# Values ahead of queries and keys in a retention mixer, two of their blocks as one double block with four sevens

## The chip, the core and the metric

The kernel runs on one core of a Trainium2 chip. TensorE (PE) multiplies matrices into PSUM; VectorE (DVE) and ScalarE (ACT) do elementwise work; GpSimd (POOL) takes a small part; SyncE (SP) issues most DMAs from HBM into SBUF. The metric is the device time in microseconds of one execution, the median of the runs.

## The reference

A decoder layer on 256 tokens of 2048 features, in float32: a half SwiGLU FFN, two token mixers side by side (retention over 8 heads, attention over a window of 128), a second half FFN, and a gated embedding, each followed by a layer norm. The change is in the retention mixer:

```
rq, rk, rv, rg, aq, ak, av, gate_r, gate_a = jnp.split(h @ w_in[i], SPLIT_POINTS, axis=-1)
rq = rotary(rq ...); rk = rotary(rk ...) * RET_DK ** -0.5
ro = head_group_norm(retention_chunkwise(rq, rk, rv), ret_gn_g[i])
ret_branch = (jax.nn.silu(rg) * ro) @ w_ret_out[i]
```

`rq` and `rk` have 1024 features each, the values `rv` 2048 (8 heads of 256). All of them are products of the same 256 x 2048 activations with columns of `w_in`. Queries, keys and values don't depend on each other; retention needs all three.

## The kernel before, in words

**A product.** Every float32 operand is split into a high part (rounded to the format that TensorE takes, `fp32r`, by an ACT cast, L98) and a low part (the rest, by a DVE subtraction, L99). A product is three matmuls: high by low, high by high, low by high (`Sum.add`, L393 to L395). Weights come in *chunks* of 128 x 1024 numbers, 512 KB; for values a chunk is two slices of 128 rows by 512 columns. A chunk against the two halves of the tokens is 12 matmuls of 512 columns.

**Pairs and sevens.** A *pair* is two slices of rows against two blocks of 512 columns and two halves of tokens, thus a 2 x 2 by 2 x 2 product of tiles. Plain ("P") it takes two chunks and 24 matmuls. A *seven* ("S", class `Seven`, L167) uses seven products in place of eight, 21 matmuls. It needs four sums of weight tiles (DVE, L189 to L192), the splits of both (class `Seven.make`), and on the left side four sums of activation tiles, the *forms* (`forms_of`, `whole` L478, `seven_forms` L466 to L469, and their split); one set of forms serves two sevens. After the last seven of a block, `seven_common` folds the shared products (ACT L500, DVE L501 to L504), and a last sum adds the plain part (L1438). `units_of("PPSSPSSP", (0, 1, 2, 3))` gives the order of units in a block and which row pairs are sevens. `mixer_block` runs such a double block; before, it serves the attention gates (`ga0`, `ga1`) and the retention output.

**The planner.** All weight units stand in one list, `plan`, in the order of their use (`plan_mixers` for this stage). `fill` moves them along: it issues loads (SyncE) while the queue of units, in units of time, is below `far`, and prepares them (ACT and DVE) while the prepared queue is below `ahead`, and only while slots are left: there are 46 slots of SBUF, and `slots_for_weights(n, ahead=45, far=90)` says how many the weights may hold. A single chunk counts 12, a seven 21. `done` frees a unit's slots and calls `fill`; so the instructions of preparing are written to DVE and ACT, which work in order, at that place of the program. During a layer norm `quiet` stops preparing; when the norm's last event "go" comes, the next `fill` prepares as much as the queue allows: 88 units after the first FFN (`last_ahead` 136, less 12 for each of 4 held chunks, in `held_out`).

**Lazy jobs.** Each unit used calls `run_side`, which also advances the first generator in `lazy` by a step. In this stage these are `sums_ahead` (sums and splits for sevens of the second FFN, L257 to L269, written away to HBM) and `rotary_table("a")`.

**The stage, before.** `mixers` takes block 0 of the values (`rv0`) inside the norm (`norm.first`, six chunks, then two more), splits the result into high and low slots (`values`, which the retention products read), and starts the lazy jobs. Then come eight groups of queries and keys (`rqk`, four chunks each, L344 and L352), each rotated on DVE (L1088 to L1098) into four slots `rq` and `rk`, the DMAs of the decay table (L1179), then values blocks 1, 2 and 3 one by one with `tokens_out`, each split from PSUM by `values`. Retention scores (L1193) begin one chunk into the next stage, `rg`.

Of the kernel before, what the change touches and what calls it, by code (L numbers as in the profile page):

```python
# [15 lines left out]
P = 128  # L16
# [39 lines left out]
def layer(ctx: ExitStack, tc: tile.TileContext, io):  # L56
# [13 lines left out]
    def banks(name):  # L70
        return [bank(name + str(j)) for j in range(2)]

    def slot(shape, dt, name):
        return slots.tile(shape, dt, tag="slot", name=name)
# [22 lines left out]
    def split(dst_hi, dst_lo, src, lo_engine=None):  # L97
        act.copy(dst_hi, src)  # L98
        (lo_engine or dve).tensor_tensor(dst_lo, src, dst_hi, ALU.subtract)  # L99
# [138 lines left out]
    def sums_ahead(items, wait, every):  # L238


        def pause():
            for _ in range(every):
                yield

        pairs = [[Chunk(k) for k in items[0]]]
        for _ in range(wait):
            yield
        for j, (key, _) in enumerate(items):
            a, b = pairs.pop()
            b11, b21, b12, b22 = a.of(a.raw, 0), a.of(a.raw, 1), b.of(b.raw, 0), b.of(b.raw, 1)  # L250
            u, v = (slot([P, 2, 512], F32, w + a.name) for w in "uv")
            t1, t3, t2, t4 = (x.rearrange("p (g n) -> p g n", g=2) for x in (u[:, 0], u[:, 1], v[:, 0], v[:, 1]))
            parts = [slot([P, 2, 512], F32R, w + a.name) for w in ("hu", "lu", "hv", "lv")]
            uh, ul, vh, vl = parts
            away = [dram.tile([P, 2, 512], F32, name=f"{w}{a.name}") for w in ("hud", "lud", "hvd", "lvd")]
            put_by_sums[key] = away
            dve.tensor_tensor(t1, b11, b12, ALU.add)  # L257
            dve.tensor_tensor(t3, b12, b22, ALU.add)
            yield from pause()
            act.copy(uh, u)  # L260
            dve.tensor_tensor(t2, b11, t3, ALU.add)
            dve.tensor_tensor(t4, t2, b21, ALU.add)
            yield from pause()
            act.copy(vh, v)
            if j + 1 < len(items):
                pairs.append([Chunk(k) for k in items[j + 1]])
            dve.tensor_tensor(ul, u, uh, ALU.subtract)
            yield from pause()
            dve.tensor_tensor(vl, v, vh, ALU.subtract)  # L269
            for e in range(2):  # L270
                sync.dma_start(away[e], parts[e].bitcast(F32))
            yield from pause()
            for e in range(2, 4):
                sync.dma_start(away[e], parts[e].bitcast(F32))
# [44 lines left out]
    def slots_for_weights(n, ahead=45, far=90):  # L319
        room.update(slots=n, ahead=ahead, far=far)  # L320
# [84 lines left out]
    def tokens_out(key, n_k, lhs, ps, n=512, before=None):  # L405

        nk = 1024 // n
        sums = [Sum(ps[t][:, :n], n_k) for t in range(2)]
        for c in range(n_k // nk):
            u = take(key + (c,))  # L410
            tokens_chunk(u.chunk, c * nk, lhs, sums, (0, 1), range(nk))
            done(u)
            run_side()
# [11 lines left out]
    def block(name, units, keys, lhs, forms, sums, fold, before=None):  # L425


        sevens = [p for kind, p in units if kind in "SD"]
        if sevens:
            p1, p6, p7, q5 = (Sum(bank(f"{name}s{j}"), len(sevens)) for j in range(4))  # L430
        for j, (kind, p) in enumerate(units):
            if before is not None:
                before(j)
            if kind in "PF":
                for n in range(2):
                    u = take(keys(n, p))
                    tokens_chunk(u.chunk, 2 * p, lhs, [sums[t][n] for t in range(2)], (0, 1))
                    done(u)
                    run_side()
                continue  # L440
            u = take(keys(0, p))
            a11, a12 = (half_of(lhs(2 * p + e), 0) for e in range(2))
            a22 = half_of(lhs(2 * p + 1), 1)
            f5, f6, f7, f3 = forms(p)
            q2, q3, q4 = sums[0][0], sums[0][1], sums[1][0]
            steps = [
                (p1, a11, u.b11), (q2, a12, u.b21), (q3, f3, u.b22), (q5, f5, u.t1),
                (p7, f7, u.t3), (p6, f6, u.t2), (q4, a22, u.t4),
            ]
            if p == sevens[-1]:  # L450
                steps = [steps[j] for j in (0, 3, 5, 4, 1, 2, 6)]
            for to, left, right in steps:
                to.add(left, right)
            done(u)
            run_side()
            if p == sevens[-1]:
                fold(p1.ap, p6.ap, p7.ap, q5.ap)
# [27 lines left out]
    def units_of(order, sevens, ahead=()):  # L485

        sevens, ahead = list(sevens), list(ahead)
        plain = [p for p in range(KD // 2) if p not in sevens + ahead]
        of = {"S": sevens, "D": ahead, "P": plain, "F": plain}
        return [(kind, of[kind].pop(0)) for kind in order]  # L490

    def block_sums(ps, units, n_k):

        s = sum(kind == "S" for kind, p in units)
        return [[Sum(ps[t][n], n_k - (2 * s if t and n else s)) for n in range(2)] for t in range(2)]
# [16 lines left out]
    def plan_tokens(key, n_k, nk=2):  # L512
        for c in range(n_k // nk):
            plan.append(Single(key + (c,)))
# [587 lines left out]

    GATE_UNITS = units_of("PPSSPSSP", (0, 1, 2, 3))
    RET_UNITS = units_of("PPPSPSPP", (0, 1))
    gate_keys = lambda b: lambda n, p: ("w_in_f2", 29 + 4 * b + 2 * n, p)
    ret_keys = lambda b: lambda n, p: ("w_ret2", 4 * b + 2 * n, p)

    def plan_mixers():
        plan_tokens(("w_rv", 0), KD)
        for grp in range(8):  # L1110
            plan_features([("w_in_f", grp)], KD)
        for blk in range(1, 4):
            plan_tokens(("w_rv", blk), KD)
        for grp in range(8, 16, 2):
            plan_tokens(("w_in_f2", grp), KD)
        plan_tokens(("w_av",), KD, nk=4)
        for grp in (20, 16, 17, 18, 19):
            plan_features([("w_in_f", grp)], KD)
        for grp in range(21, 29, 2):
            plan_tokens(("w_in_f2", grp), KD)  # L1120
        for b in range(2):
            block_units(GATE_UNITS, gate_keys(b))
        for j in range(0, 8, 2):
            plan_tokens(("w_att2", j), KD // 2)
        for b in range(2):
            block_units(RET_UNITS, ret_keys(b))
        for blk in range(4):
            plan_tokens(("w_mix", blk), KD)
# [7 lines left out]
    def mixers(ht, norm, residual, keepers, away):  # L1136
        cos_r, sin_r = trig["r"]
        rhs = lambda k: (ht[:, k, :S], ht[:, k, S:])
        both_halves = lambda k: ht[:, k, :]
        rq = [slot([P, 4, S], F32, f"rq{j}") for j in range(2)]  # L1140
        rk = [slot([P, 4, S], F32, f"rk{j}") for j in range(2)]

        def rotated(grp, ps):
            who = (rq, rk)[grp // 4][grp % 4 // 2]
            rotate(ps, f"rr{grp}", who[:, grp % 2 * 2 : grp % 2 * 2 + 2, :], cos_r, sin_r, SH_R)

        rv = []

        def values(blk, ps):
            hi, lo = (slot([P, 2, 512], F32R, f"rv{w}{blk}") for w in "hl")  # L1150
            for t in range(2):
                split(hi[:, t], lo[:, t], ps[t])
            rv.append((hi, lo))

        ps = banks("rv0")
# [7 lines left out]
            tokens_chunk(u.chunk, 2 * c, rhs, [sums[t][0] for t in range(2)], (0, 1))  # L1163
            done(u)
        values(0, ps)
        slots_for_weights(14)
        ahead = [(gu_keys("f2", j)(0, p), gu_keys("f2", j)(1, p)) for j in AHEAD for p in AHEAD[j]]
        lazy.append(sums_ahead(ahead[:2], 3, 2))
        lazy.append(rotary_table("a"))
        lazy.append(sums_ahead(ahead[2:5], 2, 2))  # L1170
        lazy.append(sums_ahead(ahead[5:8], 2, 3))
        for grp in range(8):
            ps = banks(f"rqk{grp}")
            features_out([(("w_in_f", grp), ps)], KD, both_halves)
            rotated(grp, ps)
        grp = 8
        decay = [slot([P, 2, 384], F32, f"dec{j}") for j in range(4)]
        for j in range(4):
            act.dma_start(decay[j], io["decay"][:, 2 * j : 2 * j + 2, :])  # L1179
        for blk in range(1, 4):  # L1180
            ps = banks(f"rv{blk}")
            tokens_out(("w_rv", blk), KD, rhs, ps)
            values(blk, ps)

        ret_t = [None] * HR
        gate_v = [None] * HR
        keep = {}
# [223 lines left out]
        for grp in (18, 19):  # L1411
            attention_features(grp)

        made = {}
        forms = lambda p: made[p // 2](p % 2)
        slots_for_weights(18)
        sig = []
        for j in range(4):
# [8 lines left out]
            for t in range(2):  # L1427
                act.copy(sig[-1][:, t], ps[t])
        assert not side

        def mixer_block(name, units, keys, lhs):

            ps = [banks(name + w) for w in "ab"]
            got = []
            block(name, units, keys, lhs, forms, block_sums(ps, units, KD), lambda *a: got.extend(seven_common(*a)))
            for n in range(2):
                for t in range(2):
                    dve.tensor_tensor(got[n][:, t], got[n][:, t], ps[t][n], ALU.add)  # L1438
            return got

        slots_for_weights(22)
        for b in range(2):
# [375 lines left out]
```

## Time and profile before

| | |
|---|---|
| runs (3) | median 2270.05 us, 2269.02 to 2270.55 |
| the profiled execution | 2269.44 us, its span 2267.3 us |
| mean granted TensorE clock | 0.999 |
| values block 0, from its first matmul | 706.2 us |
| queries and keys | 730.3 to 819.7 us |
| values blocks 1 to 3 | 819.7 to 885.0 us |
| gate double blocks | 1165.8 to about 1247 us |

Rows of the timeline read: start, duration, engine, line, operation, output <- inputs, shapes, count; in brackets, how long the engine had been idle and what released it. Rows of windows read: the stretch and its length, then busy time (and instructions) of PE, PE's weight loads, DVE, ACT and POOL, the granted clock, the share of the DMA engines and GB/s. Rows of waits read: who waited for whom, us in total, times, the longest.

### The profile page before, as it was taken

How to read it: one execution, taken by the hardware profiler on the slowest of the kernel's cores; microseconds unless marked ns; L12 is line 12 of the kernel's file. 1: busy time of each engine (PE TensorE's matmuls, PEld its weight loads, DVE VectorE, ACT ScalarE, POOL GpSimd, SP SyncE). 2: the span in 40 equal slices, each digit the busy share in tenths (PEclk: the TensorE clock that was granted, in tenths of full speed). 3: DMA queues.
4: the chain of work that ended last, by engine and by line, in shares of the span. 5: the costliest groups of instructions: out<-in, count | busy, mean ns of one | idle time of the engine just before them, and what ended most of it. 6: DMA issues, size and time to landing. Idle time of an engine off the chain costs nothing.

```text
span 2267.3 us, 29270 instructions
## 1 busy us (share of the span) xinstructions
PE 2258.9 (100%) x10482; PEld 1877.7 (83%) x10482; DVE 1975.9 (87%) x2576; ACT 1272.5 (56%) x1543; POOL 37.1 (2%) x49
## 2 busy tenths in 40 slices
PE   9999999999999999999999999999999999999998
PEld 7888888888888888888778888888888888888887
DVE  7988989999989887888789788689999999889887
ACT  6676776656555444535566454455555565555543
POOL 0000010000000000000000000000000000000000
PEclk9999999999999999999999999999999999999999
DMA  9888898865677878775456568787867766555772
GB/s 316 249 261 252 238 262 243 250 208 186 216 285 261 291 282 289 256 236 183 140 158 225 183 211 293 271 288 247 297 242 250 255 197 218 196 190 209 290 269 73
DMA packets 216889, 536.69 MB, mean 237 GB/s; under 512 B 17052, under 2 KB 21532, under 8 KB 216744
## 3 DMA queue, kind: packets, MB, share of 16 engines
q1 hardware_dynamic: 209000, 511.28, 65.9%
q0 software_dynamic: 5760, 20.97, 5.1%
q10 hardware_dynamic: 1984, 2.58, 0.4%
q8 instruction: 82, 1.34, 0.2%
q14 instruction: 63, 0.52, 0.1%
HBM read 484.43 MB, written 29.36 MB: 227 GB/s over the span
## 4 chain that ended last, share of the span: by engine, by line
PE 78%; DVE 1%; DMA 1%; ACT 0%; issue 0%; ACTq 0%; DVEq 0%
PE f2g L395 3%; PE f2g L393 3%; PE f2g L394 3%; PE rqk L344 3%; PE f2u L393 2%; PE f2u L395 2%; PE f2u L394 2%; PE aqk L344 2%; PE f1d L395 2%; PE f2d L394 2%; PE f2d L395 2%; PE f1d L393 2%; PE f1d L394 2%; PE f2d L393 2%; PE f1e L395 1%; PE f2e L394 1%
## 5 line engine op out<-in xcount | busy, mean ns | idle before, releaser
L99 DVE TENSOR_TENSOR lf_gu<-rf_gu,hf_gu 128x1024 fp32r<-128x1024 f32 (+1 forms) x229 | 271.9, 1210 | 11.1 <-ACT hf_gu L98 10.4
L98 ACT CAST hf_gu<-rf_gu 128x1024 fp32r<-128x1024 f32 (+1 forms) x229 | 232.8, 1041 | 30.2 <-DMA rf_gu<-in_f_gu 29.9
L99 DVE TENSOR_TENSOR lf_down<-rf_down,hf_down 128x1024 fp32r<-128x1024 f32 x150 | 178.8, 1220 | 19.0 <-ACT hf_down L98 18.5
L99 DVE TENSOR_TENSOR lw_in_f<-rw_in_f,hw_in_f 128x1024 fp32r<-128x1024 f32 x140 | 167.5, 1220 | 25.0 <-ACT hw_in_f L98 24.7
L98 ACT CAST hf_down<-rf_down 128x1024 fp32r<-128x1024 f32 x150 | 151.7, 1049 | 50.7 <-DMA rf_down<-in_f_down 18.0
L98 ACT CAST huf_gu<-uf_gu 128x1024 fp32r<-128x1024 f32 x75 | 79.0, 1053 | 147.5 <-DVE uf_gu L190 138.0
L98 ACT CAST hw_in_f<-rw_in_f 128x1024 fp32r<-128x1024 f32 x140 | 140.3, 1050 | 3.2 <-PE rv L394 1.4
L98 ACT CAST hvf_gu<-vf_gu 128x1024 fp32r<-128x1024 f32 x75 | 79.1, 1055 | 31.7 <-DVE vf_gu L192 30.8
L99 DVE TENSOR_TENSOR luf_gu<-uf_gu,huf_gu 128x1024 fp32r<-128x1024 f32 x75 | 91.4, 1219 | 0.0
L99 DVE TENSOR_TENSOR lvf_gu<-vf_gu,hvf_gu 128x1024 fp32r<-128x1024 f32 x75 | 91.4, 1218 | 0.0
L393 PE MATMUL f1g<-hf_gu,xt 128*128 128x512 f32 x232 | 90.6, 390 | 0.2 <-ACT hf_gu L98 0.2
L395 PE MATMUL f1g<-lf_gu,xt 128*128 128x512 f32 x232 | 90.7, 391 | 0.0
L394 PE MATMUL f1g<-hf_gu,xt 128*128 128x512 f32 x232 | 90.4, 390 | 0.0
L393 PE MATMUL f2g<-hf_gu,ht 128*128 128x512 f32 x217 | 84.7, 390 | 0.0
L395 PE MATMUL f2g<-lf_gu,ht 128*128 128x512 f32 x217 | 84.7, 390 | 0.0
L394 PE MATMUL f2g<-hf_gu,ht 128*128 128x512 f32 x217 | 84.5, 390 | 0.0
L994 ACT ACTIVATE eve<-eve 128x1024 f32<-128x1024 f32 x20 | 21.2, 1061 | 100.4 <-DVE eve L993 100.4
L395 PE MATMUL f1u<-lf_gu,xt 128*128 128x512 f32 x192 | 75.0, 390 | 0.7 <-DMA lf_gu<-rf_gu 0.7
L393 PE MATMUL f1u<-hf_gu,xt 128*128 128x512 f32 x192 | 75.7, 394 | 0.0
L394 PE MATMUL f1u<-hf_gu,xt 128*128 128x512 f32 x192 | 74.9, 390 | 0.0
L393 PE MATMUL f2u<-hf_gu,ht 128*128 128x512 f32 x172 | 68.2, 397 | 0.0
L395 PE MATMUL f2u<-lf_gu,ht 128*128 128x512 f32 x172 | 67.1, 390 | 0.0
(1468 smaller groups left out, 6734.7 us busy)
## 6 DMA issues: line engine op xcount, KB each, us to landing
rf_gu<-in_f_gu SPq DMA_DIRECT2D x360, 512.0 KB
rf_down<-in_f_down SPq DMA_DIRECT2D x176, 512.0 KB
rw_in_f<-in_w_in_f SPq DMA_DIRECT2D x148, 512.0 KB
lf_gu<-rf_gu POOLq DMA_DIRECT2D x40, 512.0 KB, 7.0
rw_rv<-in_w_rv SPq DMA_DIRECT2D x32, 512.0 KB
rw_ret<-in_w_ret SPq DMA_DIRECT2D x32, 512.0 KB
rw_mix<-in_w_mix SPq DMA_DIRECT2D x32, 512.0 KB
rw_pg<-in_w_pg SPq DMA_DIRECT2D x32, 512.0 KB
```

The costliest lines, as they stand in the source:

```text
L98: act.copy(dst_hi, src)
L99: (lo_engine or dve).tensor_tensor(dst_lo, src, dst_hi, ALU.subtract)
L344: pe.matmul(ps[f], hi[:, kk, f * P : (f + 1) * P], rhs(k), start=k == 0, stop=k == n_k - 1,)
L393: pe.matmul(o, al, bh, start=first, stop=False)
L394: pe.matmul(o, ah, bh, start=False, stop=False)
L395: pe.matmul(o, ah, bl, start=False, stop=self.left == 0)
L994: act.activation(g, g, AF.Silu)
```

## The change

Block 0 of the values stays. Blocks 1 and 2 become one double block of eight pairs, two plain, two sevens, one plain, two sevens, one plain, run right after block 0; block 3 follows as it was; queries and keys come after all values. Two sets of forms are made inside the double block, at its first two units. The weights have 24 slots during the double block, and 14 from block 3 on. The slots of `rq` and `rk` are taken only after the values; the decay table's DMAs stay behind the last q/k group. `mixer_block` moves up in the function and takes a `before`; `values` takes either two PSUM banks or a finished slot.

```
+    VALUE_UNITS = units_of("PPSSPSSP", (0, 1, 2, 3))
+    value_keys = lambda n, p: ("w_rv", 1 + n, p)
     def plan_mixers():
         plan_tokens(("w_rv", 0), KD)
+        block_units(VALUE_UNITS, value_keys)
+        plan_tokens(("w_rv", 3), KD)
         for grp in range(8):
             plan_features([("w_in_f", grp)], KD)
-        for blk in range(1, 4):
-            plan_tokens(("w_rv", blk), KD)
...
         values(0, ps)
-        slots_for_weights(14)
         ahead = [(gu_keys("f2", j)(0, p), gu_keys("f2", j)(1, p)) for j in AHEAD for p in AHEAD[j]]
         lazy.append(sums_ahead(ahead[:2], 3, 2))
...
+        def before_values(j):
+            if j < 2:
+                made[j] = forms_of([ht[:, 4 * j : 4 * j + 4, :]], f"rvf{j}")
+
+        for n, v in enumerate(mixer_block("rvs", VALUE_UNITS, value_keys, rhs, before_values)):
+            values(1 + n, v)
+        made.clear()
+        slots_for_weights(14)
+        ps = banks("rv3")
+        tokens_out(("w_rv", 3), KD, rhs, ps)
+        values(3, ps)
+        rq[:] = [slot([P, 4, S], F32, f"rq{j}") for j in range(2)]
+        rk[:] = [slot([P, 4, S], F32, f"rk{j}") for j in range(2)]
         for grp in range(8):
             ps = banks(f"rqk{grp}")
             features_out([(("w_in_f", grp), ps)], KD, both_halves)
...
-        for blk in range(1, 4):
-            ps = banks(f"rv{blk}")
-            tokens_out(("w_rv", blk), KD, rhs, ps)
-            values(blk, ps)
-
```

More of the change, by code (lines that the diff above doesn't have):

```diff
@@ L1139, in mixers @@
         both_halves = lambda k: ht[:, k, :]
-        rq = [slot([P, 4, S], F32, f"rq{j}") for j in range(2)]
-        rk = [slot([P, 4, S], F32, f"rk{j}") for j in range(2)]
+        rq, rk = [None] * 2, [None] * 2
         def rotated(grp, ps):
@@ L1147, in mixers, with mixer_block @@
         rv = []
+        made = {}
+        forms = lambda p: made[p // 2](p % 2)
+        def mixer_block(name, units, keys, lhs, before=None):
+            ps = [banks(name + w) for w in "ab"]
+            got = []
+            block(name, units, keys, lhs, forms, block_sums(ps, units, KD), lambda *a: got.extend(seven_common(*a)), before)
+            for n in range(2):
+                for t in range(2):
+                    dve.tensor_tensor(got[n][:, t], got[n][:, t], ps[t][n], ALU.add)
+            return got
         def values(blk, ps):
             hi, lo = (slot([P, 2, 512], F32R, f"rv{w}{blk}") for w in "hl")
-            for t in range(2):
-                split(hi[:, t], lo[:, t], ps[t])
+            if isinstance(ps, list):
+                for t in range(2):
+                    split(hi[:, t], lo[:, t], ps[t])
+            else:
+                split(hi, lo, ps)
             rv.append((hi, lo))
@@ L1412, in mixers @@
             attention_features(grp)
-        made = {}
-        forms = lambda p: made[p // 2](p % 2)
         slots_for_weights(18)
@@ L1429, in mixers @@
         assert not side
[L1431 to L1439, printed above, removed]
         slots_for_weights(22)
```

## The prediction, on record before the result

> **What bounds the kernel now.** I read the page first: busy shares, then the waits of TensorE, then stages by windows, then the timelines of single engines where the change acts.
>
> ```profile
> span 2267.3 us, 29270 instructions
> PE 2258.9 (100%) x10482; PEld 1877.7 (83%) x10482; DVE 1975.9 (87%) x2576; ACT 1272.5 (56%) x1543; POOL 37.1 (2%) x49
> ```
>
> ```profile
> PE warm L1697 <- POOL ident masks.py:199: 1.4, 1, 1.4
> PE f1u L395 <- DMA lf_gu<-rf_gu: 0.7, 1, 0.7
> ```
>
> TensorE is never without work: its two longest waits of the whole span are 1.4 and 0.7 us. A busy row alone would not prove that it runs at its pace, so I take the pace from matmul starts in the values stage, which is what the change edits, with the end of block 0 there too:
>
> ```profile
> 730.12 0.39 PE L395 MATMUL rv<-lw_rv,ht 128*128 128x512 f32 x1
> 730.34 0.84 PE L344 MATMUL rqk<-ht,hw_in_f 128*128 128x512 f32 x3
> ...
> 819.72 0.39 PE L393 MATMUL rv<-hw_rv,ht 128*128 128x512 f32 x1
> 844.89 0.39 PE L393 MATMUL rv<-hw_rv,ht 128*128 128x512 f32 x1
> ```
>
> From the third to the fourth row lie 111 matmuls of 512 columns, one after another: 25.17 / 111 = 0.2268 us each. Values already run at that pace, so matmuls taken away are time taken away, and any wait put into TensorE's order is time added. The order of blocks is neutral for TensorE as such. VectorE (DVE) is next with 87%, and where the mixers use sevens it has almost nothing left:
>
> ```profile
> 706.00:730.20 24.20, 24.20 (x118) 20.05 (x117) 20.67 (x32) 14.01 (x21) 0.00 (x0) 1.00 0.79 295
> 1165.00:1206.00 41.00, 41.00 (x186) 33.79 (x186) 39.31 (x48) 25.97 (x31) 0.00 (x0) 1.00 0.64 205
> 1206.00:1247.00 41.00, 41.00 (x182) 33.96 (x182) 40.45 (x49) 26.66 (x29) 0.00 (x0) 1.00 0.67 221
> ```
>
> The columns after the length are PE, PEld, DVE, ACT, POOL. The last two rows are the two gate blocks, built by the same `mixer_block` with the same order PPSSPSSP that the change gives the values. DVE is busy 39.3 and 40.5 of 41 us there, and TensorE does not wait. So such a block fits only just, and only with nothing else on DVE.
>
> **What the change removes.** A plain pair is 24 matmuls, a seven 21. Four sevens save 12 matmuls: 12 x 0.2268 = **2.7 us**. Two plain blocks are 192 matmuls, 43.5 us; the double block has 180, four pairs of 5.44 us and four sevens of 4.76, 40.8 us together.
>
> **What it adds on DVE.** Only DVE's order matters, so I follow it from the moment the norm lets the planner go on:
>
> ```profile
> 723.90 2.36 DVE L99 TENSOR_TENSOR lw_rv<-rw_rv,hw_rv 128x1024 fp32r<-128x1024 f32 x2 [0.26 <-ACT hw_rv L98]
> 726.18 6.90 DVE L99 TENSOR_TENSOR lw_in_f<-rw_in_f,hw_in_f 128x1024 fp32r<-128x1024 f32 x6
> 732.99 1.28 DVE L99 TENSOR_TENSOR rvl<-rv,rvh 128x512 fp32r<-128x512 f32 x2
> 734.19 2.35 DVE L99 TENSOR_TENSOR lw_in_f<-rw_in_f,hw_in_f 128x1024 fp32r<-128x1024 f32 x2
> ```
>
> Before, the burst prepares 8 chunks in 9.09 us (1.136 each), then the split of block 0 takes 1.20. `fill` stops at 88 units of queue here (136 less 4 held chunks of 12); counting its rule over the new plan gives 2 + 4 plain chunks (72 units) and then the first seven (93). So in the new kernel DVE has the six chunks by 723.90 + 6.82 = 730.72. What a seven costs is in the first gate block:
>
> ```profile
> 1167.14 0.69 DVE L189 TENSOR_TENSOR uw_in_f<-rw_in_f,rw_in_f 128x512 f32<-128x512 f32 x1
> 1169.81 1.22 DVE L99 TENSOR_TENSOR lw_in_f<-rw_in_f,hw_in_f 128x1024 fp32r<-128x1024 f32 x1
> 1172.68 1.22 DVE L99 TENSOR_TENSOR lvw_in_f<-vw_in_f,hvw_in_f 128x1024 fp32r<-128x1024 f32 x1
> 1173.81 0.69 DVE L189 TENSOR_TENSOR uw_in_f<-rw_in_f,rw_in_f 128x512 f32<-128x512 f32 x1
> ...
> 1195.09 1.22 DVE L99 TENSOR_TENSOR lvw_in_f<-vw_in_f,hvw_in_f 128x1024 fp32r<-128x1024 f32 x1
> ```
>
> One seven takes 1173.81 - 1167.14 = 6.67 us of DVE for 4.76 us of TensorE; the split of its own first chunk comes 2.67 in. And the forms of the activations, which the gate blocks got earlier, during `gt`, now stand in the block itself, at its first two units:
>
> ```profile
> 1112.69 1.22 DVE L478 TENSOR_TENSOR gaf0w<-ht 128x1024 f32<-128x1024 f32 x1
> 1113.94 0.42 DVE L466 TENSOR_TENSOR sums<-gaf0w 128x256 f32<-128x256 f32 x1
> 1116.61 1.23 DVE L99 TENSOR_TENSOR gaf0l<-sums,gaf0h 128x1024 fp32r<-128x1024 f32 x1 [1.11 <-ACT gaf0h L98]
> 1117.75 1.22 DVE L99 TENSOR_TENSOR lw_in_f<-rw_in_f,hw_in_f 128x1024 fp32r<-128x1024 f32 x1
> ```
>
> A set of forms holds DVE from 1112.69 to 1117.75 = 5.06 us (with 1.11 idle for ScalarE's cast); two sets are 10.12. The lazy preparation of sums for the second FFN now steps along in this block. By its pauses (3 steps, then one part every 2) its parts at steps 4 and 6 come ahead of the fourth seven; they look like this in the old values stage:
>
> ```profile
> 825.85 0.69 DVE L257 TENSOR_TENSOR uf_gu<-rf_gu,rf_gu 128x512 f32<-128x512 f32 x1
> 827.06 2.35 DVE L99 TENSOR_TENSOR lw_rv<-rw_rv,hw_rv 128x1024 fp32r<-128x1024 f32 x2
> 829.33 0.69 DVE L261 TENSOR_TENSOR vf_gu<-rf_gu,uf_gu 128x512 f32<-128x512 f32 x1
> 830.66 2.35 DVE L99 TENSOR_TENSOR lw_rv<-rw_rv,hw_rv 128x1024 fp32r<-128x1024 f32 x2
> ```
>
> That is 1.21 and 1.33 us (from the first row of each pair to the second).
>
> **The sum on DVE**: 730.72; first seven 737.39; split of block 0 738.59; first forms 743.65; second forms 748.71; second seven 755.38; plain chunk and lazy part 757.73; plain chunk 758.87; third seven 765.54; lazy part 766.87; fourth seven 773.54.
>
> **Against TensorE**, block start 730.34. (1) The first seven starts at 741.2 and uses the forms' low part at its third product, 742.6; it is there at 743.7: wait **1.2**. (2) The second seven could start at 747.2 and needs its first low part at its third matmul, 747.65; DVE has it at 748.71 + 2.67 + 1.22, about 752.7: wait **5.0**. (3) The plain pair and the third seven just make it (762.75 against 762.9). (4) The fourth seven starts at 767.2: first low part wanted 767.65, there 770.8 (wait 3.2); the last, wanted 1.8 us after its start as delayed and then again by the one before, there 773.6: **4.6** in all. Sum of waits **10.8**.
>
> A check that does not depend on where each wait falls: in the first gate block the fourth seven's last low part is done at 1195.09 + 1.22 = 1196.31 and used here:
>
> ```profile
> 1165.77 0.50 PE L393 MATMUL ga0a<-hw_in_f,ht 128*128 128x512 f32 x1
> 1198.35 0.39 PE L395 MATMUL ga0s<-lvw_in_f,gaf1h 128*128 128x512 f32 x1
> ```
>
> So that block has 2.0 us to spare, and its first seven begins on DVE 1.37 after the block's start; in the new block 0.38. To spare: 3.0. Added: 1.20 + 10.12 + 2.54 = 13.9. Backlog 10.9. Whatever the order of these items, the fourth seven comes after all of them.
>
> Behind the block DVE has the fold (4 operations), four sums from PSUM and two splits: by the durations shown at most 8 x 0.69 + 2 x 1.14 = 7.8 us, beside chunks and lazy parts. The fifth chunk of block 3 would be ready near 791.3 and is wanted at 793, so I cost that at nothing; if that cover is gone, 1 to 2 us. The q/k stage itself, its rotations and the lazy jobs are the same as before. DMAs: as many as before; the values' chunks are loaded in the queue places of the q/k chunks, and what late chunks would cost is within the range below. Free slots: the double block may hold 24 for weights, the gate blocks ran on 22 with no wait, so nothing. The decay table, issued right after the last q/k group, was 67 us ahead of its use and is now some 3:
>
> ```profile
> L1197 DVE TENSOR_TENSOR rsc<-rs,dec x8: 418/423/425, 888.6 to 995.9; 128x256 f32<-128x256 f32 x8
> L1179 ACTq DMA_DIRECT2D dec<-in_decay x4: 334/442/445, 819.9 to 821.3; - x4
> ```
>
> No row shows its landing. Bounds: nothing, since DVE is four chunks (10.9 us) ahead there, up to some 4 us; I take nothing.
>
> Net: -2.7 + 10.8 = **+8.1 us**. The profiled execution took 2269.44 (its span 2267.3 and 2.1 around it), giving 2277.6; on the median of 2270.05 it is 2278.2. I take **2278**.
>
> **The rivals.**
>
> *The clock after a wait.* TensorE would idle 3 to 4 us at a stretch twice. The nearest rows are matmuls that follow the start of the program:
>
> ```profile
> 5.11 0.50 PE L393 MATMUL f1g<-hf_gu,xt 128*128 128x512 f32 x1
> 5.45 0.40 PE L394 MATMUL f1g<-hf_gu,xt 128*128 128x512 f32 x1
> 5.84 0.50 PE L395 MATMUL f1g<-lf_gu,xt 128*128 128x512 f32 x1
> 6.17 0.39 PE L393 MATMUL f1g<-hf_gu,xt 128*128 128x512 f32 x1
> ```
>
> Three take 1.06 us, 0.353 each, 0.127 over the pace. If the last 18 matmuls of the fourth seven ran so, 2.3 us more (after the second seven a slow spell is swallowed by the later wait): 2280. With the plain pair too, 5.3 more. Chance 0.11. The Trainium skill, page "TensorE: Matmul & The Clock Gate", section "Why this matters for your kernels", speaks for it: a TensorE that idles more than about 3 us between bursts goes back to half clock. With the window of 3.4 us that Part 1 of that page gives, it would add an estimated 1.7 us after the fourth seven, thus about 2280. No wait in this trace is long enough to show it.
>
> *Part of the backlog is not met.* If ScalarE's casts leave DVE no gap (2 x 1.11) and the lazy parts (2.54) land behind the fourth seven, the waits are 6.0: 2270.05 - 2.7 + 6.0 = 2273. For it: the planner's lead varies. Against: both places follow from the written order. Chance 0.13.
>
> *The cover holds: not slower.* One mechanism: the burst begins earlier than 723.90, while the norm still runs, so that DVE's lead swallows the backlog. It decides from 10.8 us of lead; then only the 2.7 remain: 2267. For it: the gate blocks ran the same order with no wait. Against: the window 706.00:730.20 has DVE busy 20.67 of 24.20, so at most 3.5 us are there. Chance 0.06.
>
> **How the numbers follow.** Forecast (2274.6 to 2280) 0.66; the slow clock (2279 to 2284) 0.11; late chunks or decay, or too short a cover behind the block (2280 to 2284), 0.04; part of the backlog (2270 to 2274.6) 0.13; the cover holds (2266 to 2268) 0.06. A measurement of this kernel tells about 0.2% (4.5 us) from no change. Slower by more than that, above 2274.6: 0.66 + 0.11 + 0.04 = 0.81. Within: 0.17. Faster by over 0.2%: 0.02, taken from the cover's case, since the saved matmuls themselves are only 0.12%. The range leaves out the cover's case, the lower half of the partial one and the ends of the slow ones: 2271.5 to 2284.
>
> **What would show it.** Right: in the changed kernel TensorE waits on `rvf0l` about 1 us, on the second seven's `lw_rv` about 5, on the fourth seven's low parts about 4 to 5; DVE without a gap from 724 to 774; the stretch from the end of block 0 to block 3 about 51.7 us instead of 40.8; the other stages as long as before. Wrong: no waits of TensorE over 1 us there (the cover holds), waits on DMA, or matmuls spaced over 0.23 us after a wait (the clock).

## The result and the profile after

| | before | after |
|---|---|---|
| median of 6 runs | 2269.92 us (2269.02 to 2270.63) | 2278.61 us (2277.9 to 2278.94) |
| ratio, 95% interval | | 1.0037 [1.0025, 1.0049] |
| the profiled execution, its span | 2269.44, 2267.3 us | 2278.02, 2276.2 us |
| first matmul of values block 0 | 706.22 us | 706.83 us |
| first matmul of stage `rg` | 885.01 us | 894.06 us |

The kernel became 8.7 us slower; the forecast was 2278. The page's span and busy shares of after:

```profile
span 2276.2 us, 29321 instructions
PE 2260.6 (99%) x10470; PEld 1876.3 (82%) x10470; DVE 2004.7 (88%) x2618; ACT 1281.2 (56%) x1552; POOL 37.1 (2%) x49
```

TensorE has the 12 matmuls less that the change promises (10482 to 10470), yet its span is longer: the time went into waits. The view of TensorE's waits, after (in us: total, times, longest):

```profile
PE rvss L395 <- DVE lw_rv L99: 4.4, 2, 3.4
PE warm L1708 <- POOL ident masks.py:199: 1.4, 1, 1.4
PE rvss L393 <- ACT hw_rv L98: 1.0, 1, 1.0
PE rvsa L393 <- DVE rvf0l L99: 1.0, 1, 1.0
PE f1u L395 <- DMA lf_gu<-rf_gu: 0.9, 1, 0.9
PE rvss L395 <- DVE luw_rv L99: 0.8, 1, 0.8
```

`warm` and `f1u` were there before; the other rows are new, and all of them stand in the double block (its tiles in PSUM are `rvsa`, `rvsb` and `rvss`), for things that VectorE and ScalarE prepare. The windows of after, cut at block 0, the double block, block 3 and the queries and keys:

```profile
706.80:731.00 24.20, 24.20 (x117) 19.98 (x116) 20.66 (x32) 13.71 (x21) 0.00 (x0) 1.00 0.81 300
731.00:782.70 51.70, 44.34 (x181) 34.59 (x179) 48.75 (x62) 27.33 (x31) 0.00 (x0) 0.93 0.60 201
782.70:804.70 22.00, 22.00 (x99) 18.22 (x98) 21.96 (x24) 12.15 (x13) 0.00 (x0) 1.00 0.77 285
804.70:894.10 89.40, 89.40 (x514) 78.69 (x513) 80.81 (x120) 41.76 (x56) 0.00 (x0) 1.00 0.82 284
```

Only the second row has PE below its length: 44.34 of 51.70. It ends one matmul early; block 3 begins in this row of PE's timeline:

```profile
782.92 0.39 PE L393 MATMUL rv<-hw_rv,ht 128*128 128x512 f32 x1
```

The double block's first matmul starts at 731.02, so the stage is 51.9 us long. The two plain blocks that it replaces would take 43.5 at the pace of the prediction, so this one stage costs 8.4 us. That is all of the 8.4 by which the way from block 0 to `rg` grew (894.06 - 706.83 = 187.23, against 885.01 - 706.22 = 178.79). The same row has a second mark: a granted clock of 0.93, where all others have 1.00.

Where TensorE stands, one matmul after another, in the timeline of PE, after:

```profile
744.40 0.50 PE L393 MATMUL rvsa<-bw_rv,rvf0l 128*128 128x512 f32 x1 [0.98 <-DVE rvf0l L99]
...
749.15 0.50 PE L393 MATMUL rvss<-hw_rv,ht 128*128 128x512 f32 x1 [1.04 <-ACT hw_rv L98]
749.49 0.40 PE L394 MATMUL rvss<-hw_rv,ht 128*128 128x512 f32 x1
753.33 0.79 PE L395 MATMUL rvss<-lw_rv,ht 128*128 128x512 f32 x1 [3.44 <-DVE lw_rv L99]
753.92 0.63 PE L393 MATMUL rvsa<-hw_rv,ht 128*128 128x512 f32 x1
754.35 0.63 PE L394 MATMUL rvsa<-hw_rv,ht 128*128 128x512 f32 x1
...
757.33 0.50 PE L395 MATMUL rvss<-luw_rv,rvf0h 128*128 128x512 f32 x1
757.67 0.40 PE L393 MATMUL rvss<-huw_rv,rvf0l 128*128 128x512 f32 x1
...
771.53 0.50 PE L395 MATMUL rvss<-lw_rv,ht 128*128 128x512 f32 x1 [0.96 <-DVE lw_rv L99]
...
773.26 0.50 PE L395 MATMUL rvss<-luw_rv,rvf1h 128*128 128x512 f32 x1 [0.78 <-DVE luw_rv L99]
...
774.40 0.50 PE L395 MATMUL rvss<-lvw_rv,rvf1h 128*128 128x512 f32 x1 [0.16 <-DVE lvw_rv L99]
```

First seven (744.40), second (749.15, 753.33), none in the third, fourth (from 771.53). Read the starts behind 753.33 too: 753.92 to 757.33 are 8 steps, 0.43 us each, nearly twice the 0.2268 us of a matmul at pace, though nothing is waited for. The clock goes with it, by two windows of after:

```profile
749.00:753.00 4.00, 0.73 (x2) 0.30 (x2) 3.86 (x6) 2.50 (x4) 0.00 (x0) 0.72 0.18 73
753.00:758.00 5.00, 4.67 (x12) 3.72 (x13) 5.00 (x7) 3.58 (x5) 0.00 (x0) 0.54 0.00 2
```

After an idle stretch of 3.44 us the granted clock is 0.54 for the next 5 us, and 0.2268 / 0.43 is 0.53. What TensorE waited for is in DVE's timeline, after:

```profile
743.12 1.23 DVE L99 TENSOR_TENSOR rvf0l<-sums,rvf0h 128x1024 fp32r<-128x1024 f32 x1 [1.12 <-ACT rvf0h L98]
744.26 1.22 DVE L478 TENSOR_TENSOR rvf1w<-ht 128x1024 f32<-128x1024 f32 x1
...
749.33 0.69 DVE L189 TENSOR_TENSOR uw_rv<-rw_rv,rw_rv 128x512 f32<-128x512 f32 x1
...
752.05 1.22 DVE L99 TENSOR_TENSOR lw_rv<-rw_rv,hw_rv 128x1024 fp32r<-128x1024 f32 x1
...
757.20 0.68 DVE L257 TENSOR_TENSOR uf_gu<-rf_gu,rf_gu 128x512 f32<-128x512 f32 x1
...
766.27 0.68 DVE L261 TENSOR_TENSOR vf_gu<-rf_gu,uf_gu 128x512 f32<-128x512 f32 x1
...
767.60 0.69 DVE L189 TENSOR_TENSOR uw_rv<-rw_rv,rw_rv 128x512 f32<-128x512 f32 x1
...
773.13 1.21 DVE L99 TENSOR_TENSOR lvw_rv<-vw_rv,hvw_rv 128x1024 fp32r<-128x1024 f32 x1
```

The first forms are done at 744.35. The second set holds DVE from 744.26 to 749.33; then come the second seven, a lazy part, and so on to the fourth seven's last low part, done at 774.34. TensorE's last wait ends right behind that, at 774.40.

### The profile page after: what moved, and what is told of

It reads as the page before. It is cut to its first block, busy times and chain, and to the rows that moved or that the text cites. A ratio compares the mean times of both kernels' runs of the same rounds, so it can differ in the third digit from the quotient of the medians.

```text
span 2276.2 us, 29321 instructions
## 1 busy us (share of the span) xinstructions
PE 2260.6 (99%) x10470; PEld 1876.3 (82%) x10470; DVE 2004.7 (88%) x2618; ACT 1281.2 (56%) x1552; POOL 37.1 (2%) x49
## 4 chain that ended last, share of the span: by engine, by line
PE 76%; DVE 2%; ACT 1%; DMA 1%; issue 0%; ACTq 0%; DVEq 0%
PE f2g L395 3%; PE f2g L393 3%; PE f2g L394 3%; PE rqk L344 3%; PE f2u L393 2%; PE f2u L395 2%; PE f2u L394 2%; PE aqk L344 2%; PE f2d L393 2%; PE f1d L394 2%; PE f2d L394 2%; PE f1d L395 2%; PE f1d L393 2%; PE f2d L395 2%; PE f2e L395 1%; PE f2e L393 1%
## 5 line engine op out<-in xcount | busy, mean ns | idle before, releaser
L99 DVE TENSOR_TENSOR lf_gu<-rf_gu,hf_gu 128x1024 fp32r<-128x1024 f32 (+1 forms) x229 | 272.0, 1210 | 11.5 <-ACT hf_gu L98 10.3
L99 DVE TENSOR_TENSOR lf_down<-rf_down,hf_down 128x1024 fp32r<-128x1024 f32 x150 | 178.8, 1220 | 19.9 <-ACT hf_down L98 19.6
```

## The experiments

**Theory.** DVE is the feeder, and its backlog at the fourth seven (its work up to there less its lead) comes out as lost time of TensorE one for one, mostly because of the two sets of forms. **Rivals**: the new order itself, or the decay table behind it, costs time; the loss is in the clock after a wait; the loss is in where the sevens stand. All ratios below are against the kernel before, run beside each (its medians there were 2269.67 to 2270.09 us). Differences from the changed kernel are between medians of separate measurements, whose intervals reach 2 to 3.5 us to either side; the length of the double block in the traces, given beside several of them, tells more.

| run | median, us | ratio, 95% |
|---|---|---|
| order alone | 2269.53 | 0.9999 [0.999, 1.0008] |
| no forms | 2268.06 | 0.9993 [0.9984, 1.0001] |
| forms twice | 2288.62 | 1.0084 [1.0069, 1.01] |
| lazy jobs behind the block | 2278.24 | 1.0037 [1.0024, 1.0049] |
| forms on GpSimd | 2279.83 | 1.0044 [1.003, 1.0058] |
| plain pairs first | 2281.01 | 1.0049 [1.0036, 1.0062] |
| double block at the old place | 2282.87 | 1.0054 [1.0037, 1.0071] |
| matmuls by zeros in the wait | 2279.68 | 1.0043 [1.003, 1.0056] |
| two sevens | 2268.32 | 0.9993 [0.9984, 1.0001] |

**1. The order alone.** All four value blocks plain, ahead of queries and keys.

```
-        block_units(VALUE_UNITS, value_keys)
-        plan_tokens(("w_rv", 3), KD)
+        for blk in range(1, 4):
+            plan_tokens(("w_rv", blk), KD)
...
+        for blk in range(1, 4):
+            ps = banks(f"rv{blk}")
+            tokens_out(("w_rv", blk), KD, rhs, ps)
+            values(blk, ps)
```

> The order alone: all four value blocks plain, ahead of queries and keys; no sevens among the values. Theory (DVE's backlog in the double block is the loss, the order is neutral): 2269.9 us, within 1 us of the kernel before, no wait of TensorE over 0.5 us in this stage. Rival (the move itself costs, by the late decay table or by the lazy jobs in another place): 2274 us or more.

Measured: no difference, and from block 0 to `rg` the 178.8 us of before. The move costs nothing, and neither does the decay table, which has the same place here. That rival is out.

**2. No forms.** The sevens take plain slices of the activations in the forms' place.

```
-                made[j] = forms_of([ht[:, 4 * j : 4 * j + 4, :]], f"rvf{j}")
+                made[j] = lambda e: [(ht[:, 4 * j + e, :P], ht[:, 4 * j + e, S : S + P])] * 4
```

> The changed kernel without the forms: the left sides of the sevens are plain slices of the activations, so the sums of activations are left out and the values come out wrong; all matmuls are there. Theory: 10.1 us less on DVE, backlog 10.9 - 10.1 = 0.8, so 2269.9 - 2.7 + 0.8 = 2268.0 us, waits 0 to 1.5 us. Rival (sevens with the lazy jobs are already too much for DVE here): 2273 us or more.

Measured: 10.5 us less than the changed kernel, for 10.12 us of forms taken from DVE; the double block takes 41.9 us in place of 51.9. TensorE's waits without the forms:

```profile
PE rvss L395 <- DVE luw_rv L99: 0.3, 1, 0.3
PE rvss L395 <- DVE lvw_rv L99: 0.2, 1, 0.2
```

The other waits in the block are gone; what is left is the last bit of the backlog, at the fourth seven. Against the kernel before, even this is no gain that the interval can tell (0.9993 [0.9984, 1.0001]).

**3. The forms twice.** Each set is computed twice, and the second copy used.

```
-                made[j] = forms_of([ht[:, 4 * j : 4 * j + 4, :]], f"rvf{j}")
+                for e in "xf":
+                    made[j] = forms_of([ht[:, 4 * j : 4 * j + 4, :]], f"rv{e}{j}")
```

> The changed kernel with each set of forms computed twice on DVE (the first is not used). Theory: 10.1 us more on DVE ahead of the fourth seven are 10.1 us more of waits: 2288.5 us. Rival (the waits have another cause, or part of them is the clock): less than 2284 us.

Measured: 10.0 us more than the changed kernel, for 10.12 us of DVE put in; the double block takes 62.1 us in place of 51.9. Together with the run before, the rate is one us per us in both directions. Where it lands has shifted, in the waits with the forms twice:

```profile
PE rvsa L393 <- DVE rvf0l L99: 6.2, 1, 6.2
PE rvss L393 <- ACT hw_rv L98: 3.7, 1, 3.7
PE rvss L395 <- DVE lw_rv L99: 3.4, 2, 2.9
```

The first seven now waits 6.2, where it waited 1.0. The sum follows DVE's backlog; the place follows the order of its work.

**4. The lazy jobs behind the block.** The four `lazy.append` lines are moved behind the double block, so that no sums for the second FFN are prepared in it.

```
-        lazy.append(sums_ahead(ahead[:2], 3, 2))
...
             values(1 + n, v)
+        lazy.append(sums_ahead(ahead[:2], 3, 2))
```

> The changed kernel with the lazy jobs begun only behind the double block. Theory: 2.54 us less on DVE ahead of the fourth seven, so about 2276.1 us, and the waits in the block about 8.5 us. Rival (the wait is set by the forms' and the second seven's place alone, or the clock after the wait decides): 2278 us or more, unchanged.

Measured: the median is only 0.4 us below the changed kernel, so the expected total was missed. In the trace the block and block 3 together did become shorter as expected, 71.3 us in place of 73.7. The view of waits shows where that went:

```profile
PE rvss L395 <- DVE lw_rv L99: 3.4, 1, 3.4
PE at L1398 <- DVE asc L1388: 1.6, 1, 1.6
```

Of the fourth seven's waits only one of 0.2 us (on `lvw_rv`) is left, and a wait that the changed kernel doesn't have stands in attention (`at`, behind the scores' elementwise work). The lazy parts are late there now: DVE still does six of their operations from 1041.0 on (L257 to L269), among the rotation and the scores, where the last in the changed kernel begins at 1032.7. From the first matmul of attention's queries and keys (`aqk`) to the first of stage `gt` is 62.7 us, against 60.6. At the first gate double block (`ga0a`) nothing is left of the gain: from block 0's first matmul to there both traces take 468.1 us, to within 0.1. So all of the 2.4 is given back. Moved work still has to be done somewhere.

**5. The forms on GpSimd.** The five sums and the low part of each set run on the engine that is otherwise idle.

```
-        split(hi, lo, raw)
+        split(hi, lo, raw, eng)
...
-                made[j] = forms_of([ht[:, 4 * j : 4 * j + 4, :]], f"rvf{j}")
+                made[j] = forms_of([ht[:, 4 * j : 4 * j + 4, :]], f"rvf{j}", pool)
```

> The changed kernel with the forms computed on GpSimd instead of DVE (five sums and the low part; the high part stays on ScalarE). Theory: DVE is rid of 10.1 us as in the run without forms, 2268 us if GpSimd is done in time and doesn't slow DVE; up to 2272 us if it does. Rival (the backlog is not DVE's work but the forms' place ahead of the sevens): 2276 us or more, with waits on the forms.

Measured: 1.2 us above the changed kernel; the expectation was wrong. The double block takes 53.1 us in place of 51.9. Taking 10 us from DVE did not help, and the timelines of DVE, GpSimd and ScalarE of this run show two reasons:

```profile
725.97 9.03 DVE L99 TENSOR_TENSOR lw_rv<-rw_rv,hw_rv 128x1024 fp32r<-128x1024 f32 x6 [0.26 <-ACT hw_rv L98]
745.11 2.88 DVE L190 TENSOR_TENSOR uw_rv<-rw_rv 128x512 f32<-128x512 f32 x1
```

```profile
742.24 2.40 POOL L99 TENSOR_TENSOR rvf0l<-sums,rvf0h 128x1024 fp32r<-128x1024 f32 x1 [10.60 <-ACT rvf0h L98]
744.60 2.84 POOL L479 TENSOR_TENSOR rvf1w<-ht 128x1024 f32<-128x1024 f32 x1
```

```profile
751.69 1.04 ACT L98 CAST rvf1h<-sums 128x1024 fp32r<-128x1024 f32 x1 [9.53 <-POOL sums L470]
```

First, GpSimd and ScalarE work in order: the second set's sums stand behind the first set's low part, for which GpSimd waited 10.60 us; ScalarE waited 9.53 for those sums, and the second seven's high part is queued behind that cast. Hence the longest wait of TensorE in this run:

```profile
PE rvss L393 <- ACT hw_rv L98: 5.1, 1, 5.1
```

Second, DVE is stretched while GpSimd works: a sum of 128x512 that took 0.69 us takes 2.88 beside GpSimd's 2.84. The six low parts take 9.03 us, while GpSimd is busy with the first set's sums up to 731.6; the changed kernel has them in this row of its DVE timeline:

```profile
724.52 6.90 DVE L99 TENSOR_TENSOR lw_rv<-rw_rv,hw_rv 128x1024 fp32r<-128x1024 f32 x6 [0.26 <-ACT hw_rv L98]
```

That agrees with the Trainium skill, page "SBUF — State Buffer", section "Who interferes with whom": a DVE instruction with two SBUF inputs contends with a GpSimd instruction that reads SBUF. GpSimd was not a free engine for this work.

**6. Plain pairs first.** The same four sevens, after all four plain pairs.

```
-    VALUE_UNITS = units_of("PPSSPSSP", (0, 1, 2, 3))
+    VALUE_UNITS = units_of("PPPPSSSS", (0, 1, 2, 3))
```

> The changed kernel with the order PPPPSSSS: the same work on every engine, but TensorE has all four plain pairs ahead of the sevens. Theory: TensorE reaches the last seven 5.4 us later, DVE has 2.3 us of plain chunks and 1.1 us of a lazy part more ahead of it; waits 8.8 us instead of 11, none on the first seven, about 2.4, 1.9 and 4.5 on the others: 2275.8 us. Rival (only the sum of work counts, not its order): 2278.5 us.

Measured: 2.4 us above the changed kernel, 5.2 above the expectation and 2.5 above its rival, so neither holds as it stands. The waits, and the timeline of PE at the end of the block:

```profile
PE rvss L395 <- DVE lw_rv L99: 5.1, 2, 2.7
PE rv L393 <- DVE evw L501: 3.0, 1, 3.0
```

```profile
785.01 0.50 PE L393 MATMUL rv<-hw_rv,ht 128*128 128x512 f32 x1 [3.01 <-DVE evw L501]
785.34 0.59 PE L394 MATMUL rv<-hw_rv,ht 128*128 128x512 f32 x1
785.73 0.63 PE L395 MATMUL rv<-lw_rv,ht 128*128 128x512 f32 x1
```

In the sevens TensorE loses 9.7 us, about the 8.8 expected, though with slow matmuls in place of the wait at the third seven. What was overlooked is the last plain pair: it covers the fold. With a seven last, block 3 needs a bank of PSUM that `evw` (L501) still reads, waits 3.0 us, and then runs eight matmuls at about 0.43 us. Block 3 takes 26.7 us in place of 21.8: 4.9, nearly the 5.2 missed. The prediction's "cover behind the block" was for block 3's chunks, at 1 to 2 us if gone; this wait for the fold is another one, which it did not have.

**7. The double block alone, at the old place.** Behind queries and keys, where DVE has no burst ahead of it; the weights have 20 slots there.

```
         for grp in range(8):
             plan_features([("w_in_f", grp)], KD)
+        block_units(VALUE_UNITS, value_keys)
+        plan_tokens(("w_rv", 3), KD)
```

> The double block alone, without the move: block 0, queries and keys, then the double block with its forms inside (20 slots for weights, since the rotated queries and keys hold four), then block 3. Theory: the backlog is DVE's work ahead of the fourth seven less its lead. Here the lead is one ordinary queue of four chunks, not the norm's longer burst, the rotation of the last key group (3.5 us) stands ahead of the forms, and 3.7 us of lazy parts: the first seven is begun 9 us after the block's start instead of 0.4, waits about 14 us, 2281 us. Rival (the loss came from the place ahead of queries and keys): 2276 us or less.

Measured: 4.3 us above the changed kernel, a little more than expected. Its waits:

```profile
PE rvss L395 <- DVE lw_rv L99: 6.0, 3, 3.3
PE rvss L393 <- ACT hw_rv L98: 4.3, 1, 4.3
```

Where DVE begins the first seven, in its timeline of this run and then of the changed kernel:

```profile
829.83 0.68 DVE L189 TENSOR_TENSOR uw_rv<-rw_rv,rw_rv 128x512 f32<-128x512 f32 x1
```

```profile
731.34 0.69 DVE L189 TENSOR_TENSOR uw_rv<-rw_rv,rw_rv 128x512 f32<-128x512 f32 x1
```

That is 8.9 us after the block's first matmul here (820.89), behind the first forms, and 0.3 after it in the changed kernel (731.02). Of the 8.6 between them 3.5 are left at DVE's end of the fourth seven (46.8 us behind the block's first matmul, against 43.3), for here the first forms and the split of block 0 are already made, and one lazy part more is done. The double block grew by 4.7, to 56.6 us: the other 1.2 are slow matmuls, which come behind the fourth seven's waits here. So the two halves of the change are not alike: the sevens cost, and the place behind the norm makes them cost less.

**8. Matmuls by zeros in the wait.** 14 matmuls by a zero tile stand ahead of the second seven, so that TensorE isn't idle so long. A few lines more make the tile.

```
+            if j == 3:
+                for _ in range(14):
+                    pe.matmul(ps[0][0], zero, ht[:, 0, :], start=False, stop=False)
```

> The changed kernel with 14 matmuls by zeros (they add nothing to a sum under way) between the first and the second seven, where TensorE waits: 3.2 us of work inside the wait, so that it stands idle for at most 2 us at a stretch. Theory (the fourth seven waits for DVE's end anyway): the ten slow matmuls of the second seven go, the fourth seven waits about 2 us longer, total unchanged at 2278.5 us. Rival (the slow clock is part of the loss): 2276.5 us.

Measured: no gain, so the rival is out; 1.1 us above the changed kernel, its interval holding the changed kernel's ratio. The second seven now runs at pace. Then the fourth seven waits at one stretch, and the slow clock comes there, in the waits and the windows of this run:

```profile
PE rvss L395 <- DVE lw_rv L99: 4.5, 2, 2.9
```

```profile
768.00:772.00 4.00, 1.07 (x6) 0.57 (x4) 3.93 (x7) 2.21 (x3) 0.00 (x0) 0.90 0.85 282
772.00:778.00 6.00, 5.91 (x13) 4.19 (x14) 6.00 (x6) 6.00 (x8) 0.00 (x0) 0.50 0.06 23
```

There are 13 matmuls at 0.43 us, some 2.6 us too many. Ten of them stand behind the last wait, where nothing swallows them: the double block takes 53.6 us, against 51.9. DVE's last low part for the fourth seven is done 67.6 us after block 0's first matmul, and 67.5 in the changed kernel: the spell doesn't move DVE's end. So the slow spell in the changed kernel cost nothing: what it takes from the second seven the fourth doesn't wait.

**9. Two sevens.** The order of the retention output, with one set of forms.

```
-    VALUE_UNITS = units_of("PPSSPSSP", (0, 1, 2, 3))
+    VALUE_UNITS = units_of("PPPSPSPP", (0, 1))
...
-            if j < 2:
+            if j < 1:
```

> The changed kernel with two sevens instead of four: order PPPSPSPP, one set of forms. Theory: 13.3 us of sevens' surplus and forms go, the last seven has one plain pair of TensorE's time more ahead of it, so no wait; 6 matmuls saved, 1.4 us: about 2268.4 us. Rival (any seven with its forms inside this stage costs): 2271 us or more, with waits of 2 us or more on the first seven.

Measured: no wait of TensorE in the block at all, and 10.3 us below the changed kernel. Two sevens and a set of forms less take 2 x (6.67 - 2.27) + 5.06 = 13.9 us from DVE, more than the backlog of 10.9. Against the kernel before, the 6 matmuls saved (1.4 us) are no more than the interval can tell: 0.9993 [0.9984, 1.0001].

## Why the prediction was right, point by point

| step | forecast | in the trace |
|---|---|---|
| matmuls saved | 12 | 12 |
| wait at the first seven | 1.2 | 0.98, with the restart 1.3 |
| second seven | 5.0 | 1.04 + 3.44, with the restarts 4.9 |
| slow clock in the second seven | swallowed later | 10 matmuls, 2.1 us |
| third seven | none, 0.15 to spare | none, 2.2 to spare |
| fourth seven | 4.6 | 0.96 + 0.78 + 0.16 and restarts, 2.7 |
| sum | 10.8 | 11.1 |
| stretch to block 3 | 51.7 | 51.9 |
| DVE's end of the fourth seven | 773.6 | 774.34 |

The sum is the stretch less 180 matmuls at 0.2268. "With the restart" counts the starts of matmuls against that pace: the first step after a wait takes about 0.1 us more (0.34 from 749.15 to 749.49).

- **The feeder sets the end.** This held most exactly. Block 0 began 0.6 us later in this execution, which leaves 0.1 of the 0.7 on DVE's end. Runs 2 and 3 show the rate of one for one that the backlog check rested on.
- **The fourth seven's wait** was mis-sized, 4.6 against 2.7. The slow spell in the second seven took 2.1 us out of it, as it did out of the third seven's time to spare. The forecast's sum is right nevertheless, since the end is set by DVE and not by where TensorE loses the time; run 8 bears this out by moving the spell.
- **The clock rival** was half right. The clock did fall after a long wait, and cost 0.2 us a matmul, more than the 0.127 taken from the program's start. The part with a price, a slow spell behind the fourth seven, did not come: its waits are three short ones, the longest 0.96 us, and no matmul behind them is slow. In runs 7 and 8 it came.
- **An added ScalarE wait** (1.04 at 749.15) was not forecast. It costs nothing of its own, since the low part that TensorE wants two matmuls later comes 3.44 us after that in any case.
- **The lazy parts** lie ahead of the fourth seven, at 757.20 and 766.27, where the count of steps put them. Run 4 shows their 2.4 us in this stage, and that moving them brings nothing by the gates.
- **At nothing** were costed: the order, the decay table (run 1: nothing) and the cover behind the block. Behind the double block, the windows of after have PE busy throughout. Run 6 shows what the plain pair behind the last seven is worth, by another wait than the prediction named.
- Part of the backlog unmet, or the whole cover: neither happened.

What stays open: no run has four sevens here and is clearly faster than the kernel before, so whether they would pay with forms made elsewhere is not shown. In run 5 the two reasons were not taken apart.

## What to carry to other kernels

Where one engine feeds another, add up the feeder's work from the last moment of known lead to the last product that needs it; what is over comes out as waits, one for one in runs 2 and 3. That holds while nothing else ends later: in run 6 the order added a wait for the fold, and in run 5 the queues of two other engines took what VectorE was spared. A seven saves TensorE 0.68 us here (3 matmuls) and takes 4.4 us of VectorE more than a plain pair, and a set of forms 5.06; so it pays only where VectorE has that time, and saved matmuls alone say nothing. Keep a unit without late needs behind the last seven for the fold, and before giving work to an idle engine, follow what waits in order behind it.

## What the runs showed of the hardware

The clock fell after waits shorter than 3 us. Slow spells followed idle stretches of 3.44 us (after), 3.01 (run 6) and 2.93 (run 8); in run 6 a wait of 2.38 us did it too, with the slow matmuls beginning 1.3 us after the restart. Two waits close together also did: 2.75 and 0.48 us in run 6, 1.37 and 0.77 in run 7. Single waits of 1.6 us (run 8) and 1.36 (run 7), with busy time around them, did not. The spells took 5 to 13 matmuls at 0.43 us; over two stretches within them the granted clock was 0.54 (after) and 0.50 (run 8). The Trainium skill, page "TensorE: Matmul & The Clock Gate", section "Why this matters for your kernels", puts the idle time at more than about 3 us; these runs show the same fall to half clock, and a shorter wait that is enough for it.
